# Block sums of a seven-product matmul made by accumulating transfers

## The chip, the cores and the metric

One Trainium2 chip, one of its cores. The metric is the device time of one execution in microseconds, the median over the runs shown. Float32 data; the matmuls are made of three passes over parts of the operands (below).

## The reference

A two-layer decoder trunk on 256 tokens of width 1024. Each layer has a feed-forward block, a mixer (block attention beside a convolution, or a gating unit beside stick-breaking attention) and a second feed-forward block, each between two RMS norms. The change touches the four feed-forward blocks alone, with 2816 hidden columns:

```python
def swiglu(h, w_gate, w_up, w_down):
    return (jax.nn.silu(h @ w_gate) * (h @ w_up)) @ w_down

f = swiglu(rmsnorm(x, g[0]), ffn_w_gate[layer, 0], ffn_w_up[layer, 0], ffn_w_down[layer, 0])
x = x + 0.5 * rmsnorm(f, g[1])
```

## The kernel before

The 256 tokens are two tiles t of 128. The hidden columns are 11 chunks c of 256; a chunk's weights are the gate and the up columns side by side, 1024 rows of 512. `load` brings half a chunk (512 rows) into a buffer `raw` of 128 x 2048 floats, 1 MB, by two transfers from SyncE's queue. There are five raw buffers. `split_raw` makes two units of each: ScalarE copies 1024 columns into `hi` (rounded), VectorE takes the difference into `lo`; there are nine buffers of each. A matmul of the two is three passes on TensorE (hi by hi, hi by lo, lo by hi).

Chunks (2,3), (5,6) and (8,9) of each feed-forward are pairs, 12 in all. For a pair a, b = a + 1 the product is a 2 x 2 block matmul (token tile by row half, row half by chunk) that is made with seven products in place of eight (function `M`, steps i = 0 to 6, one product of 12 matmuls each). The weight blocks are b11, b21 (chunk a, first and second half of the rows) and b12, b22 (chunk b). Four of the seven products take sums of blocks, which VectorE makes in the raw buffers, each 128 x 2048 (lines 358, 359, 374, 382): b12 := b22 - b12, b11 := b12 + b11, then b12 := b22 - b11 and b21 := b21 - b11. The sums of the activations are made once in a feed-forward (`sums`). What the products leave in PSUM is put together by VectorE (u1, u2, c) and goes to `gated`, which applies SiLU on ScalarE and the product on VectorE; then come the transposes (`T`) and the down product (`Dn`, 12 matmuls over a chunk of w_down, whose raw buffer is split in the same way). Tiles X, Y and X2 are PSUM buffers, of which two exist.

A list G of steps is laid out by hand, and `settle` puts T and Dn steps behind the steps that made their chunk. The scheduler of the language sets the order of instructions on each engine from that at build time; each engine runs its own instructions in that order and waits on semaphores. GpSimd issues no transfers: it has the power operation of the norms (line 182), small copies and part of the convolution.

Of the kernel before, what the change touches and what calls it, by code (L numbers as in the profile page):

```python
# [10 lines left out]
F32 = mybir.dt.float32  # L11
# [37 lines left out]
def trunk(ctx, tc, x, norm_g, w_gate, w_up, w_down, ab_in, ab_out, conv_w, conv_b, conv_g, conv_bb,  # L49
# [68 lines left out]
            units += prep(loads, f"gu{l}{j}_{c}_{half}")  # L118
        return [(hi[:, o:o + 512], lo[:, o:o + 512]) for hi, lo in units for o in (0, 512)]

    def load_block(l, j, c, half):

        def loads(raw):
            v = raw.rearrange("p (k g f) -> p k g f", k=4, g=2)
            return [(v[:, :, g, :], w[l, j, half * 512:half * 512 + 512, c * FC:(c + 1) * FC].rearrange("(k p) f -> p k f", p=P))
                    for g, w in ((0, w_gate), (1, w_up))]
        return load(loads, f"b{l}{j}_{c}_{half}")

    def prep_in(w, c, name):
        units = []  # L130
# [119 lines left out]
    def ffn(l, j, pre, tail, hooks=()):  # L250
# [59 lines left out]

        S = {}

        def sums():
            (a11, a12), (a21, a22) = pre[0][3], pre[1][3]
            for n, dst, x, y, op in ((1, a22, a21, a22, ALU.add), (3, a21, a11, a21, ALU.subtract),
                                     (2, a11, a22, a11, ALU.subtract), (4, a12, a12, a11, ALU.subtract)):
                nc.vector.tensor_tensor(dst, x, y, op=op)
                d = sp.tile([P, 8, P], F32R, tag=f"S{n}" if n < 4 else "tg", name=f"S{n}_{l}{j}", bufs=1)  # L320
                split(dst, d[:, 0:4].rearrange("p a b -> p (a b)"), d[:, 4:8].rearrange("p a b -> p (a b)"))
                S[n] = (d[:, 0:4], d[:, 4:8])

# [14 lines left out]
        def M(i, a):  # L338
            b = a + 1
            n = f"{l}{j}_{a}"  # L340
            if i == 0:
                if not S:
                    sums()
                w = W[a] = {}
                w["m"] = sp.tile([P, 2, 512], F32, tag="cacc", name=f"m{n}")
                w["u"] = sp.tile([P, 2, 512], F32, tag="hpad", name=f"u{n}")
                w["b11"] = load_block(l, j, a, 0)
                units = split_raw(w["b11"], f"b11_{n}")
                w["b22"] = load_block(l, j, b, 1)
                w["b12"] = load_block(l, j, b, 0)  # L350
                w["X"] = ps_mm(f"gX{n}")
                product(w["X"], block(0, 0), units, True, False)
                nc.scalar.activation(w["m"][:, 0], w["X"], AF.Copy)
                return
            w = W[a]
            m1, m5, u1, u2 = w["m"][:, 0], w["m"][:, 1], w["u"][:, 0], w["u"][:, 1]
            if i == 1:
                nc.vector.tensor_tensor(w["b12"], w["b22"], w["b12"], op=ALU.subtract)
                nc.vector.tensor_tensor(w["b11"], w["b12"], w["b11"], op=ALU.add)
                units = split_raw(w["b11"], f"t2_{n}")  # L360
                w["b21"] = load_block(l, j, a, 1)
                w["Y"] = ps_mm(f"gY{n}")
                product(w["Y"], S[2], units, True, False)
                nc.vector.tensor_tensor(u1, w["Y"], m1, op=ALU.add)
            elif i == 2:
                units = split_raw(w["b21"], f"b21_{n}")
                product(w["X"], block(0, 1), units, False, True)
                gated(0, a, w["X"])
            elif i == 3:
                units = split_raw(w["b12"], f"t3_{n}")  # L370
                product(w["Y"], S[3], units, False, False)
                nc.vector.tensor_tensor(u2, w["Y"], m1, op=ALU.add)
            elif i == 4:
                nc.vector.tensor_tensor(w["b12"], w["b22"], w["b11"], op=ALU.subtract)  # L374
                units = split_raw(w["b12"], f"t1_{n}")
                w["X2"] = ps_mm(f"gX2{n}")
                product(w["X2"], S[1], units, True, False)
                nc.scalar.activation(m5, w["X2"], AF.Copy)
                nc.vector.tensor_tensor(u2, u2, m5, op=ALU.add)
                gated(1, b, u2)  # L380
            elif i == 5:
                nc.vector.tensor_tensor(w["b21"], w["b21"], w["b11"], op=ALU.subtract)
                units = split_raw(w["b21"], f"t4_{n}")
                product(w["Y"], block(1, 1), units, False, True)
                c = sp.tile([P, 512], F32, tag="va", name=f"c21_{n}", bufs=2)
                nc.vector.tensor_tensor(c, w["Y"], m1, op=ALU.add)
                gated(1, a, c)
            else:
                units = split_raw(w["b22"], f"b22_{n}")
                product(w["X2"], S[4], units, False, True)  # L390
                c = sp.tile([P, 512], F32, tag="va", name=f"c12_{n}", bufs=2)
                nc.vector.tensor_tensor(c, w["X2"], u1, op=ALU.add)
                gated(0, b, c)


        inside = {c for pair in pairs for c in pair}
# [5 lines left out]
            elif (c, c + 1) in pairs:  # L402
                G.extend((M, i, c) for i in range(7))
        G.append((GU, 0, e))
        makes = {2: (0, 0), 4: (1, 1), 5: (1, 0), 6: (0, 1)}
        price = {M: 1.0, GU: 2.0, both: 4.0, T: 0.1, Dn: 1.0}
        total = sum(price[f] for f, _, _ in G if f not in (T, Dn)) + 2
        seq, made, turned_, clock, gone, downs = [], [], [], 0.0, 0.0, 0
# [508 lines left out]
```

## Time and profile before

| | before |
|---|---|
| median of the runs shown | 992.99 us |
| the runs | 993.05, 986.86, 992.99 us |
| profiled execution | 989.26 us, its span 987.3 us |
| TensorE busy | 953.1 us (97%) |
| VectorE busy | 837.7 us (85%) |
| ScalarE busy | 579.4 us (59%) |
| GpSimd busy | 97.7 us (10%) |
| DMA queue of SyncE | 174.50 MB, 53.7% of the 16 engines' span |
| TensorE's granted clock, mean | 0.994 |

PE is TensorE, PEld its weight loads, DVE is VectorE, ACT ScalarE, POOL GpSimd, SP SyncE; a q behind a name is that engine's queue. Times in the trace count from the start of the span. Matmuls overlap in the pipeline, so a matmul's own time is longer than the step from one to the next.

### The profile page before, as it was taken

The page shows a single profiled execution, that of the slowest core. Times are in us where ns is not written, and L with a number is a line of the kernel's source. Part 1 is how long each engine was busy: PE and PEld are TensorE (multiplying, and loading weights), DVE is VectorE, ACT ScalarE, POOL GpSimd, SP SyncE. Part 2 cuts the span into 40 slices and gives each one's busy share as a digit, 9 for nine tenths or more (in the row PEclk, how much of TensorE's full clock was granted, in tenths as well). Part 3 has the DMA queues.
Part 4 walks back from the last instruction along what each step waited for, and adds up shares of the span by engine and source line. Part 5 has one row for each costly group of instructions (what it writes and reads, how often), then busy time and mean ns, then how long its engine had stood idle before and what let it go on. Part 6 is the DMA issues. An engine that isn't in the chain of part 4 may idle for free.

```text
span 987.3 us, 11853 instructions
## 1 busy us (share of the span) xinstructions
PE 953.1 (97%) x4350; PEld 759.0 (77%) x4352; DVE 837.7 (85%) x1022; ACT 579.4 (59%) x845; POOL 97.7 (10%) x104
## 2 busy tenths in 40 slices
PE   7999999999888999999999999999999989999997
PEld 5777888787657688878778887877787778887875
DVE  6999999679887999988789999996757489999883
ACT  7575656563535656656576756575555466656561
POOL 0100000039961000000000000000000010000000
PEclk9999999999989999999999999999999999999999
DMA  9657647456007339383862658385564142838341
GB/s 313 209 184 230 218 167 282 161 177 232 1 18 239 91 107 315 122 262 121 284 213 86 200 183 275 109 311 162 209 220 144 43 127 86 275 120 288 107 168 43
DMA packets 121754, 175.32 MB, mean 178 GB/s; under 512 B 4481, under 2 KB 96321, under 8 KB 121696
## 3 DMA queue, kind: packets, MB, share of 16 engines
q1 hardware_dynamic: 121536, 174.50, 53.7%
q8 instruction: 34, 0.56, 0.2%
q14 instruction: 24, 0.20, 0.1%
q10 hardware_dynamic: 160, 0.07, 0.0%
HBM read 173.50 MB, written 1.05 MB: 177 GB/s over the span
## 4 chain that ended last, share of the span: by engine, by line
PE 84%; DVE 8%; ACT 3%; DMA 2%; issue 2%; POOL 1%; SPq 0%; POOLq 0%; DVEq 0%; ACTq 0%
PE f L145 8%; PE f L146 8%; PE f L147 8%; PE gu L147 6%; PE gu L145 6%; PE gu L146 6%; PE gX L334 4%; PE gX L336 4%; PE gX L335 4%; PE gY L334 3%; PE gY L335 3%; PE gY L336 3%; PE hT L153 2%; PE cd L145 2%; PE cd L146 2%
## 5 line engine op out<-in xcount | busy, mean ns | idle before, releaser
L145 PE MATMUL f<-hi_dn,hs 128*128 128x512 f32 x352 | 139.7, 400 | 0.5 <-ACT hs L157 0.5
L146 PE MATMUL f<-lo_dn,hs 128*128 128x512 f32 x352 | 138.0, 392 | 0.0
L147 PE MATMUL f<-hi_dn,hs 128*128 128x512 f32 x352 | 137.5, 393 | 0.0
L96 ACT ACTIVATE hi_t<-raw_b 128x1024 fp32r<-128x1024 f32 x96 | 98.1, 1053 | 60.2 <-DVE raw_b L374 47.1
L97 DVE TENSOR_TENSOR lo_t<-raw_b,hi_t 128x1024 fp32r<-128x1024 f32 x96 | 114.5, 1220 | 14.5 <-ACT hi_t L96 14.5
L97 DVE TENSOR_TENSOR lo_dn<-raw_dn,hi_dn 128x1024 fp32r<-128x1024 f32 x88 | 105.7, 1219 | 9.0 <-ACT hi_dn L96 8.9
L96 ACT ACTIVATE hi_dn<-raw_dn 128x1024 fp32r<-128x1024 f32 x88 | 91.7, 1055 | 36.4 <-PE gu L147 26.2
L97 DVE TENSOR_TENSOR lo_gu<-raw_gu,hi_gu 128x1024 fp32r<-128x1024 f32 x80 | 96.6, 1218 | 8.3 <-ACT hi_gu L96 8.0
L96 ACT ACTIVATE hi_gu<-raw_gu 128x1024 fp32r<-128x1024 f32 x80 | 83.5, 1055 | 27.9 <-PE m L147 11.7
L97 DVE TENSOR_TENSOR lo_b<-raw_b,hi_b 128x1024 fp32r<-128x1024 f32 x72 | 86.3, 1219 | 2.5 <-ACT hi_b L96 2.3
L96 ACT ACTIVATE hi_b<-raw_b 128x1024 fp32r<-128x1024 f32 x72 | 74.8, 1057 | 21.4 <-PE gu L147 12.9
L145 PEld LDWEIGHTS f<-hi_dn,hs 128*128 128x128 f32 x352 | 65.7, 188 | 17.2 <-ACT hs L157 4.4
L147 PEld LDWEIGHTS f<-hi_dn,hs 128*128 128x128 f32 x352 | 66.1, 188 | 15.3 <-DVE hs L158 1.7
L146 PEld LDWEIGHTS f<-lo_dn,hs 128*128 128x128 f32 x352 | 66.2, 188 | 13.8 <-DVE lo_dn L97 1.0
L157 ACT ACTIVATE hs<-hT 128x256 fp32r<-128x256 f32 x88 | 32.2, 377 | 54.9 <-PE hT L153 54.9
L145 PE MATMUL gu<-hi_gu,xh_l1f 128*128 128x512 f32 x160 | 63.6, 397 | 0.0
L146 PE MATMUL gu<-lo_gu,xh_l1f 128*128 128x512 f32 x160 | 63.4, 396 | 0.0
L147 PE MATMUL gu<-hi_gu,xl_l1f 128*128 128x512 f32 x160 | 62.2, 393 | 0.0
L158 DVE TENSOR_TENSOR hs<-hT,hs 128x256 fp32r<-128x256 f32 x88 | 36.0, 418 | 20.4 <-ACT hs L157 20.0
L282 ACT ACTIVATE sg<-gu 128x256 f32<-128x256 f32 x38 | 14.5, 381 | 42.1 <-PE gu L147 39.3
L334 PE MATMUL gY<-hi_t,S 128*128 128x512 f32 x96 | 38.6, 402 | 0.0
L336 PE MATMUL gY<-hi_t,S 128*128 128x512 f32 x96 | 38.0, 396 | 0.0
(361 smaller groups left out, 2240.7 us busy)
## 6 DMA issues: line engine op xcount, KB each, us to landing
raw_dn<-in_ffn_w_down_dram SPq DMA_DIRECT2D x44, 1024.0 KB, 5.0
raw_b<-in_ffn_w_gate_dram SPq DMA_DIRECT2D x48, 512.0 KB, 4.7
raw_b<-in_ffn_w_up_dram SPq DMA_DIRECT2D x48, 512.0 KB, 6.2
raw_gu<-in_ffn_w_gate_dram SPq DMA_DIRECT2D x38, 512.0 KB, 4.2
raw_gu<-in_ffn_w_up_dram SPq DMA_DIRECT2D x38, 512.0 KB, 5.2
raw_ab<-in_ab_w_in_dram SPq DMA_DIRECT2D x10, 1024.0 KB, 6.9
raw_cd<-in_cd_w_in_dram SPq DMA_DIRECT2D x10, 1024.0 KB, 5.1
raw_abo<-in_ab_w_out_dram SPq DMA_DIRECT2D x4, 1024.0 KB, 5.5
```

The source lines that it names most:

```text
L96: nc.scalar.activation(hi, r, AF.Copy)
L97: nc.vector.tensor_tensor(lo, r, f32v(hi), op=ALU.subtract)
L145: nc.tensor.matmul(ps, xh, wh, start=first, stop=False)
L146: nc.tensor.matmul(ps, xh, wl, start=False, stop=False)
L147: nc.tensor.matmul(ps, xl, wh, start=False, stop=last)
L153: nc.tensor.transpose(ps[:, i * P:(i + 1) * P], src[:, i * P:(i + 1) * P], ident)
L157: nc.scalar.activation(hi, ps, AF.Copy)
L158: nc.vector.tensor_tensor(lo, ps, f32v(hi), op=ALU.subtract)
L282: nc.scalar.activation(sg, ps[:, 0:FC], AF.Silu, scale=1.0 if r is None else r)
L334: nc.tensor.matmul(ps, A[0][:, k, :], wh[:, o], start=first and k == 0, stop=False, **tc_skip)
L335: nc.tensor.matmul(ps, A[0][:, k, :], wl[:, o], start=False, stop=False, **tc_skip)
L336: nc.tensor.matmul(ps, A[1][:, k, :], wh[:, o], start=False, stop=k == 3, **tc_skip)
```

## The change

Of the four sums of blocks of a pair three are made by transfers that add what they bring to what lies in the destination, issued from GpSimd's queue; one stays on VectorE. Blocks and sums have other signs so that all four are additions: t = b12 + b11 (b11 is read from HBM once more), t := t + b22 (VectorE), b22 := b22 + b12 (b12 once more from HBM), b21 := b21 + t (from one raw buffer to another). All four blocks are loaded at the first step, b12 first. The products come in another order: b11, t (b12 + b11), b21, b22, t (with b22), b22 (with b12), b21 (with t). The post-sums and the order in which the outputs are made follow.

```diff
@@ -118,13 +118,21 @@
-    def load_block(l, j, c, half):
+    def block_of(l, j, c, half):
 
         def loads(raw):
             v = raw.rearrange("p (k g f) -> p k g f", k=4, g=2)
             return [(v[:, :, g, :], w[l, j, half * 512:half * 512 + 512, c * FC:(c + 1) * FC].rearrange("(k p) f -> p k f", p=P))
                     for g, w in ((0, w_gate), (1, w_up))]
-        return load(loads, f"b{l}{j}_{c}_{half}")
+        return loads
+
+    def load_block(l, j, c, half):
+        return load(block_of(l, j, c, half), f"b{l}{j}_{c}_{half}")
+
+    def add_block(raw, l, j, c, half):
+
+        for dst, src in block_of(l, j, c, half)(raw):
+            tc.keep_in_program_order(nc.gpsimd.dma_start(dst, src, accum_op=ALU.add))
@@ -310,12 +318,13 @@
-            for n, dst, x, y, op in ((1, a22, a21, a22, ALU.add), (3, a21, a11, a21, ALU.subtract),
-                                     (2, a11, a22, a11, ALU.subtract), (4, a12, a12, a11, ALU.subtract)):
+            for n, dst, x, y, op in ((1, a22, a21, a22, ALU.subtract), (3, a21, a11, a21, ALU.subtract),
+                                     (2, a11, a22, a11, ALU.subtract), (4, a12, a12, a11, ALU.add)):
@@ -338,16 +347,24 @@
+            def made(x, y, op, name):
+                c = sp.tile([P, 512], F32, tag="va", name=f"{name}_{n}", bufs=2)
+                nc.vector.tensor_tensor(c, x, y, op=op)
+                return c
+
             if i == 0:
...
+                w["t"] = load_block(l, j, b, 0)
+                add_block(w["t"], l, j, a, 0)
                 w["b11"] = load_block(l, j, a, 0)
                 units = split_raw(w["b11"], f"b11_{n}")
+                w["b21"] = load_block(l, j, a, 1)
                 w["b22"] = load_block(l, j, b, 1)
-                w["b12"] = load_block(l, j, b, 0)
...
             if i == 1:
-                nc.vector.tensor_tensor(w["b12"], w["b22"], w["b12"], op=ALU.subtract)
-                nc.vector.tensor_tensor(w["b11"], w["b12"], w["b11"], op=ALU.add)
-                units = split_raw(w["b11"], f"t2_{n}")
-                w["b21"] = load_block(l, j, a, 1)
...
+                units = split_raw(w["t"], f"t1_{n}")
+                w["X2"] = ps_mm(f"gX2{n}")
+                product(w["X2"], S[1], units, True, False)
+                nc.scalar.activation(m5, w["X2"], AF.Copy)
...
             elif i == 3:
-                units = split_raw(w["b12"], f"t3_{n}")
+                units = split_raw(w["b22"], f"b22_{n}")
+                nc.vector.tensor_tensor(w["t"], w["t"], w["b22"], op=ALU.add)
+                add_block(w["b22"], l, j, b, 0)
+                tc.keep_in_program_order(nc.gpsimd.dma_start(w["b21"], w["t"], accum_op=ALU.add))
+                product(w["X2"], S[4], units, False, True)
+            elif i == 4:
+                units = split_raw(w["t"], f"t2_{n}")
+                w["Y"] = ps_mm(f"gY{n}")
+                product(w["Y"], S[2], units, True, False)
+                nc.vector.tensor_tensor(u1, w["Y"], m1, op=ALU.add)
+                gated(0, b, made(w["X2"], u1, ALU.subtract, "c12"))
+            elif i == 5:
+                units = split_raw(w["b22"], f"t3_{n}")
                 product(w["Y"], S[3], units, False, False)
                 nc.vector.tensor_tensor(u2, w["Y"], m1, op=ALU.add)
-            elif i == 4:
-                nc.vector.tensor_tensor(w["b12"], w["b22"], w["b11"], op=ALU.subtract)
...
+                nc.vector.tensor_tensor(u2, m5, u2, op=ALU.subtract)
                 gated(1, b, u2)
-            elif i == 5:
-                nc.vector.tensor_tensor(w["b21"], w["b21"], w["b11"], op=ALU.subtract)
+            else:
                 units = split_raw(w["b21"], f"t4_{n}")
                 product(w["Y"], block(1, 1), units, False, True)
...
+                gated(1, a, made(w["Y"], m1, ALU.add, "c21"))
@@ -402,7 +413,7 @@
-        makes = {2: (0, 0), 4: (1, 1), 5: (1, 0), 6: (0, 1)}
+        makes = {2: (0, 0), 4: (0, 1), 5: (1, 1), 6: (1, 0)}
```

## Rows read from the trace of the kernel before

**Rows 1.** The page's busy time, share of the span and instructions of each engine.

```profile
PE 953.1 (97%) x4350; PEld 759.0 (77%) x4352; DVE 837.7 (85%) x1022; ACT 579.4 (59%) x845; POOL 97.7 (10%) x104
```

**Rows 2.** Busy time by stretch: length, engines in order, granted clock, DMA share, GB/s.

```profile
60.00:70.00 10.00, 8.18 (x37) 6.40 (x35) 10.00 (x8) 7.37 (x9) 0.00 (x0) 1.00 0.75 239
...
540.00:550.00 10.00, 10.00 (x45) 8.19 (x44) 9.83 (x10) 6.30 (x7) 0.00 (x0) 1.00 0.01 2
...
590.00:600.00 10.00, 10.00 (x46) 8.18 (x45) 9.50 (x9) 4.87 (x7) 0.00 (x0) 1.00 0.31 100
600.00:610.00 10.00, 10.00 (x47) 7.95 (x46) 9.80 (x12) 7.93 (x10) 0.00 (x0) 1.00 1.04 325
800.00:810.00 10.00, 7.67 (x32) 6.18 (x31) 7.01 (x11) 5.06 (x10) 2.53 (x1) 0.83 0.44 135
```

**Rows 3.** TensorE's waits: waited for, us in total, times, longest.

```profile
PE xT_l1f L153 <- ACT y_l1f L197: 3.3, 3, 2.3
...
PE gY L334 <- ACT hi_t L96: 1.8, 1, 1.8
...
PE gu L145 <- DVE c L392: 0.7, 1, 0.7
```

**Rows 4.** Chain of waits from 55 to 70 us: start, us, what.

```profile
59.55 2.20 DVE raw_b L374
...
62.35 2.21 DVE raw_b L382
```

**Rows 5.** The norms' power operation on GpSimd: ns min/median/max, first and last start.

```profile
L182 POOL TENSOR_TENSOR v_pl1f<-v_pl1f,mhalf x4: 548/548/2529, 501.2 to 801.5; 128x1 f32<-128x1 f32 x4
```

**Rows 6.** Groups by line and shape: count, busy us, mean ns, idle before, releasers.

```profile
L97 DVE TENSOR_TENSOR lo_t<-raw_b,hi_t 128x1024 fp32r<-128x1024 f32 x96 | 114.5, 1220 | 14.5 <-ACT hi_t L96 14.5
...
L96 ACT ACTIVATE hi_t<-raw_b 128x1024 fp32r<-128x1024 f32 x96 | 98.1, 1053 | 60.2 <-DVE raw_b L374 47.1 <-PE f L147 6.1 <-DVE raw_b L359 5.9
...
L97 DVE TENSOR_TENSOR lo_ab<-raw_ab,hi_ab 128x1024 fp32r<-128x1024 f32 x20 | 27.7, 1414 | 2.4 <-ACT hi_ab L96 2.4
L359 DVE TENSOR_TENSOR raw_b<-raw_b,raw_b 128x2048 f32<-128x2048 f32 x12 | 27.5, 2289 | 0.2
```

**Rows 7.** The 1 MB transfers into raw_dn, issue to landing.

```profile
DMA to landing us min/median/max: 4.8/5.0/9.5
```

**Rows 8.** The page's DMA queue of SyncE: packets, MB, share of 16 engines.

```profile
q1 hardware_dynamic: 121536, 174.50, 53.7%
```

**Rows 9.** Timeline of one pair: its first load's issue, its second product's split.

```profile
560.13 0.37 SPq L87 DMA_DIRECT2D raw_b<-in_ffn_w_gate_dram  x1
...
581.80 1.06 ACT L96 ACTIVATE hi_t<-raw_b 128x1024 fp32r<-128x1024 f32 x1
```

**Rows 10.** Timeline of VectorE: fourth splits' ends in four pairs, one last split.

```profile
54.13 2.35 DVE L97 TENSOR_TENSOR lo_t<-raw_b,hi_t 128x1024 fp32r<-128x1024 f32 x2
...
544.77 2.29 DVE L382 TENSOR_TENSOR raw_b<-raw_b,raw_b 128x2048 f32<-128x2048 f32 x1
546.97 1.22 DVE L97 TENSOR_TENSOR lo_t<-raw_b,hi_t 128x1024 fp32r<-128x1024 f32 x1
...
588.87 2.35 DVE L97 TENSOR_TENSOR lo_t<-raw_b,hi_t 128x1024 fp32r<-128x1024 f32 x2
...
609.53 1.22 DVE L97 TENSOR_TENSOR lo_b<-raw_b,hi_b 128x1024 fp32r<-128x1024 f32 x1
...
637.27 2.35 DVE L97 TENSOR_TENSOR lo_t<-raw_b,hi_t 128x1024 fp32r<-128x1024 f32 x2
```

**Rows 11.** Timeline of TensorE: the seventh product's first matmul in these pairs.

```profile
71.13 0.39 PE L334 MATMUL gX<-hi_b,S 128*128 128x512 f32 x1
...
564.09 0.39 PE L334 MATMUL gX<-hi_b,S 128*128 128x512 f32 x1
...
615.19 0.39 PE L334 MATMUL gX<-hi_b,S 128*128 128x512 f32 x1
...
660.88 0.39 PE L334 MATMUL gX<-hi_b,S 128*128 128x512 f32 x1
```

More of the change, by code (lines that the diff above doesn't have):

```diff
@@ L357, in M @@
             if i == 1:
-                nc.vector.tensor_tensor(w["b12"], w["b22"], w["b12"], op=ALU.subtract)
-                nc.vector.tensor_tensor(w["b11"], w["b12"], w["b11"], op=ALU.add)
-                units = split_raw(w["b11"], f"t2_{n}")
-                w["b21"] = load_block(l, j, a, 1)
-                w["Y"] = ps_mm(f"gY{n}")
-                product(w["Y"], S[2], units, True, False)
-                nc.vector.tensor_tensor(u1, w["Y"], m1, op=ALU.add)
+                units = split_raw(w["t"], f"t1_{n}")
+                w["X2"] = ps_mm(f"gX2{n}")
+                product(w["X2"], S[1], units, True, False)
+                nc.scalar.activation(m5, w["X2"], AF.Copy)
             elif i == 2:
@@ L369, in M @@
             elif i == 3:
-                units = split_raw(w["b12"], f"t3_{n}")
+                units = split_raw(w["b22"], f"b22_{n}")
[11 more added lines that the diff above has]
+                units = split_raw(w["b22"], f"t3_{n}")
                 product(w["Y"], S[3], units, False, False)
                 nc.vector.tensor_tensor(u2, w["Y"], m1, op=ALU.add)
-            elif i == 4:
-                nc.vector.tensor_tensor(w["b12"], w["b22"], w["b11"], op=ALU.subtract)
[L375 to L379, printed above, removed]
+                nc.vector.tensor_tensor(u2, m5, u2, op=ALU.subtract)
                 gated(1, b, u2)
-            elif i == 5:
-                nc.vector.tensor_tensor(w["b21"], w["b21"], w["b11"], op=ALU.subtract)
+            else:
                 units = split_raw(w["b21"], f"t4_{n}")
                 product(w["Y"], block(1, 1), units, False, True)
[L385 to L393, printed above, removed]
+                gated(1, a, made(w["Y"], m1, ALU.add, "c21"))
         inside = {c for pair in pairs for c in pair}
```

## The prediction

> **What bounds the kernel now.** I read the page's busy times first: TensorE is busy for 953.1 of 987.3 us, VectorE for 837.7, ScalarE for 579.4, GpSimd for 97.7 [rows 1]. No change to other engines can give back more than TensorE's 34.2 us without work, and much of that lies in the mixers and norms, which the change leaves alone. Next, the busy time by stretch: inside the pairs TensorE is busy for all of 10.00 us while VectorE is busy for 9.5 to 9.83 [rows 2]. So VectorE is nearly full there, but TensorE is full, and TensorE sets the time. Third, who waited for whom: of TensorE's waits only two can go back to what the change removes, 1.8 us behind a split that came late in the very first pair, and 0.7 us behind a post-sum that may have stood behind a block sum on VectorE [rows 3]; I count both as gained. The chain of waits shows the first: two sums of 2.2 us stand one behind the other on VectorE before the split that TensorE waits for [rows 4]; in that stretch TensorE is busy for 8.18 of 10 us [rows 2]. Last the stretch from 800 to 810 us: one GpSimd operation that usually takes 548 ns took 2529 [rows 5], TensorE waited up to 2.3 us for what followed [rows 3], and the granted clock of the stretch is 0.83 [rows 2], so the lower level, 1.2 GHz, held for about 3.4 us and cost 1.7 us more. After the wait of 1.8 us it stayed at 1.00. I take a stall over 2.5 us to cost 1.7 us extra, one under 2 us none.
>
> **What is removed.** Three of four block sums in each of 12 pairs: 36 operations of 2.29 us, 82 us of VectorE [rows 6]; the view has four lines like that one, one for each sum. They stood on VectorE, beside a full TensorE, so nearly all of it is worth nothing; what shows is the 1.8 + 0.7 = 2.5 us of waits. That is the whole gain.
>
> **What is added.** Per pair three accumulates from GpSimd's queue, in five transfers: b11 from HBM onto t (which holds b12), b12 from HBM onto b22, and t from SBUF onto b21, 1 MB each. GpSimd issues no transfer before, so no row prices one. The plain 1 MB transfer lands 4.8 us after issue at the least, 5.0 in the median [rows 7]. The big queue moved 174.50 MB in 53.7% of 987.3 us [rows 8], or 329 GB/s, so 1.05 MB keep the 16 engines busy for 3.2 us and some 1.8 us are latency. An accumulate must also read what it adds to. The lower bound is that this costs nothing; then two accumulates behind each other take 1.8 + 3.2 + 3.2 = 8.2 us. If each byte costs twice, they take 12.8 us on the engines and 1.8 us of latency; three issues at 0.37 us, the price on SP's queue [rows 9], make 1.1, and I round up to 16.0 for the loads beside them. The upper bound is that the three transfers do not overlap and that GpSimd needs 2.5 us for each order, its slowest operation [rows 5]: 3 x (1.8 + 2.5) + 12.8 = 25.7 us. I take 16.0 because reading the destination is real work on the same engines, while nothing shows that the transfers run one by one.
>
> The Trainium skill (Collectives: The Full Stack, The bandwidth ceiling) says that a reducing transfer issues two reads per chunk and so runs at half the rate of a copy, measured there as 1.93; by it the 12.8 us would be 12.4, and no run here shows it yet.
>
> The first accumulate (onto t) has time. A pair's first load is issued at 560.13 and its second product's split begins at 581.80 [rows 9]; t now has that first load, and 21.7 us hold a plain landing of 5 us and an accumulate of 1.8 + 6.4 us, with 8 to spare. I price it at nothing; the first product and the split before it cover it, and if that cover were gone it would cost 8.2 us a pair.
>
> The other two are the ones that count. They can start only when the fourth product's split (of b22) has read b22, and b22 and b21 are due for the sixth and seventh product. So I ask how long the time between is. The end of the fourth split is VectorE's lo operation; the seventh product's first matmul is TensorE's row; a first half of a split takes 1.05 + 1.22 us before it [rows 6]. TensorE's times stay, since it is full.
> - First pair of a feed-forward (three of them alike): the lo ends at 546.97 + 1.22 = 548.2, with a sum of 2.29 ahead of it that is gone, so 545.9 to 546.4 [rows 10]; the seventh product starts at 564.09 [rows 11]. 564.1 - 2.3 - 546.4 = 15.4 us. If the remaining sum (t + b22, 2.29 us) comes behind the split, 13.1. I take the middle, 14.2.
> - The very first pair: 54.13 + 2.35 = 56.5 [rows 10] to 71.13 [rows 11]: 12.3 or 10.1, middle 11.2.
> - Last pairs (four): 637.27 + 2.35 = 639.6 to 660.88 [rows 10, 11]: 19.0 or 16.7, middle 17.8.
> - Middle pairs (four): 588.87 + 2.35 = 591.2 to 615.19: 21.7 or 19.4, middle 20.5.
>
> With 16.0 us the seventh split is late by 1.8 us in three pairs, by 4.8 us in the very first, and in time in eight: 10.2 us. While ScalarE waits for b21, the turned-and-split operations of the down products stand behind it in its queue, so TensorE has nothing to put in the place. Only the 4.8 us stall is over 2.5 and costs 1.7 us of clock. The gain that stays is 0.7 us, for the 1.8 us lies in the pair that is now late. Sum: 10.2 + 1.7 - 0.7 = +11.2 us.
>
> Edits with no price: signs of the post-sums and their order are the same number of VectorE operations of the same shapes; the PSUM buffers X, X2, Y are held as long as before in mirror image. On GpSimd only the next pair's accumulates and the norms' power operations are queued behind an accumulate's wait; the norms come after the last down products, when the pairs are over. VectorE slows beside GpSimd: the same split took 1414 ns in the stretch where GpSimd was busy throughout, and 1220 elsewhere [rows 6]; 16% of VectorE's time in 12 times 16 us is 31 us, hidden in the 82 us freed.
>
> The profiled execution took 989.3 us in all, 2.0 around its span of 987.3; the runs shown are 986.9, 993.0 and 993.1, the median 3.7 above the profiled one. I set the sum on 991, between the two: 991 + 11 = 1002.
>
> **The rivals.**
> - Hidden anyway (not slower). If an accumulate costs little more than a plain transfer (8.2 us) or up to 13 us, every window but the very first pair's holds it, and the kernel gains up to 2.5 us: 988.5. For it: the engines that move data are used at 53.7% [rows 8], at 0.01 to 0.31 where tight and middle windows begin [rows 2]. Against: the destination must be read. It decides below about 14 us.
> - Late in every pair. Midway between 16.0 and 25.7, at 21 us, the lateness is 6.8 in three pairs, 9.8 in the first, 3.2 in four, 0.5 in four: 45; eight stalls over 2.5 us add 13.6 of clock: +58, so 1049. At the upper bound it is 11.5, 14.5, 7.9 and 5.2: 101 and 20 of clock, 1111. For it: 1 KB pieces, and descriptors that GpSimd has to write; against: nothing in the trace shows either as slow.
> - The DMA engines become the bound in bursts. From 590 to 610 us they are busy for 0.31 and 1.04 of the time [rows 2], 13.5 of 20 us; 12.8 more are 6.3 too many. Loads and accumulates then delay each other, and the lead of the last split over its product, 615.2 - (609.5 + 1.2) = 4.4 us [rows 10, 11], covers all but 2. Over eight pairs 16 us, on top of some 10 in the first ones: 1017.
> - GpSimd's norm operations turn slow behind transfers, as the one of 2529 ns [rows 5] did: 2 us and 1.7 of clock at each of four places, 15 us: 1006.
>
> The Trainium skill (DMA: Bandwidth & Descriptors, Issuing engines are not separate DMA queues) says that transfers of all queues run on the same 16 engines and interleave; by that the third rival is a matter of the share left free, which the rows of the stretch give.
>
> **How the numbers follow.** Hidden 0.28; late in the first pairs (the forecast) 0.37; late in every pair 0.17; bursts 0.11; slow norms 0.04; a better order found by chance, over 1% faster, 0.03, since only 2.5 us of waits can go. About 1%, 10 us, is what a measurement here can tell from no change. The forecast's +11 lies at that line; I give 0.20 of its 0.37 to slower. Slower: 0.20 + 0.17 + 0.11 + 0.04 = 0.52; same: 0.28 + 0.17 = 0.45; faster: 0.03. The range runs from 985 (hidden, on a fast run) to 1055 (the nearer half of late in every pair; the farther half, under 0.1, is left out); the forecast alone spans 992 to 1015.
>
> **What would show it.** VectorE's busy time falls by about 82 us to 755, with 12 sums of 2.29 us left. GpSimd's queue shows 60 transfers (five in each of 12 pairs), 38 MB more in all. The waits show ScalarE's hi split standing behind a transfer onto raw_b, and TensorE behind that split, in the four first pairs: then the step on the windows is right. It is wrong if the time from issue to landing of the b22 and b21 accumulates together is under 13 us (hidden) or over 20 (all pairs), if the waits lie at plain loads (bursts), or if t, which I priced at nothing, is the one waited for. A lower granted clock in the middle of a feed-forward would show stalls over 2.5 us.

## The result, and the profile after

The changed kernel takes 1090.95 us (1087.62 to 1098.89) where the one before, beside it, takes 990.88: a ratio of 1.103, 95% interval 1.095 to 1.110. That is 100 us slower, against a forecast of 11 and a range that ended at 1055.

The profiled execution has a span of 1088.4 us against 987.3, 101.1 more. Its page, busy times and queues (as in [rows 1, 8]), and the granted clock (before 0.994):

```profile
PE 981.0 (90%) x4352; PEld 772.1 (71%) x4352; DVE 763.1 (70%) x986; ACT 582.1 (53%) x845; POOL 170.9 (16%) x164
...
q1 hardware_dynamic: 121536, 174.50, 48.0%
q0 software_dynamic: 27072, 37.75, 20.5%
```

```profile
core 0: 1088.4 us, clock 0.965
```

VectorE lost its 36 sums (1022 to 986 operations, 74.6 us of busy time). q0 is GpSimd's new queue. TensorE runs the same matmuls, but its busy time grew from 953.1 [rows 1] to 981.0 us: 27.9 of the 101.1 us are matmuls that run slower, in stretches at the lower clock (13 in the trace against 3 before). Its idle time grew from 34.2 to 107.4 us, by the other 73.2. Nearly all of that is the first three waits below, 72.4 us together; the same three were 0.9 us before. TensorE's and ScalarE's waits after (waited for, us in total, times, longest):

```profile
PE gY L343 <- DVE u L393: 39.0, 12, 9.2
PE f L153 <- ACT hs L165: 17.0, 4, 5.7
PE hT L161 <- DVE h L293: 16.4, 12, 3.6
...
ACT hi_t L96 <- DMA raw_b<-in_ffn_w_up_dram: 59.5, 12, 8.7
ACT hi_dn L96 <- DMA raw_dn<-in_ffn_w_down_dram: 51.5, 8, 8.7
...
ACT hi_t L96 <- DMA raw_b<-raw_b: 29.3, 12, 3.6
```

Below, A is the transfer that makes T1 (b11 onto t), B the one for T3 (b12 onto b22), C the one for T4 (t onto b21). TensorE never waits for T3's or T4's own split here: it waits for hs, h and u, small operations of ScalarE and VectorE. ScalarE waits for B 5 us in each of 12 pairs, for C 2.4, and 51.5 us for down weights, plain loads that wait in line.

A first pair, timeline of all engines (start, length, engine, line, operation; in brackets the idle time before and what ended it):

```profile
391.02 1.30 POOL L135 DMA_DIRECT2D raw_b<-in_ffn_w_gate_dram  x1 [28.92 <-DVE lo_b L97]
...
391.77 1.86 POOL L135 DMA_DIRECT2D raw_b<-in_ffn_w_up_dram  x1
...
392.53 2.01 POOL L387 DMA_DIRECT2D raw_b<-raw_b  x1
...
392.85 0.37 SPq L87 DMA_DIRECT2D raw_gu<-in_ffn_w_gate_dram  x1
...
399.73 0.39 PE L345 MATMUL gX<-hi_b,S 128*128 128x512 f32 x1
403.51 2.00 ACT L96 ACTIVATE hi_t<-raw_b 128x1024 fp32r<-128x1024 f32 x2 [8.66 <-DMA raw_b<-in_ffn_w_up_dram]
...
405.42 0.36 ACT L165 ACTIVATE hs<-hT 128x256 fp32r<-128x256 f32 x1
...
405.83 0.79 PE L153 MATMUL f<-hi_dn,hs 128*128 128x512 f32 x1 [5.71 <-ACT hs L165]
...
408.68 2.00 ACT L96 ACTIVATE hi_t<-raw_b 128x1024 fp32r<-128x1024 f32 x2 [2.90 <-DMA raw_b<-raw_b]
```

T3's split waits for B until 403.51, 12.5 us after its issue. The hs of a down product, whose transposes were done at 397, stands behind it on ScalarE, and TensorE is idle from 400.1 to 405.8. C is there at 408.68, 17.7 us after B's issue. The engines' share in that time (length, engines' busy times, granted clock, DMA share, GB/s):

```profile
389.00:391.00 2.00, 2.00 (x10) 1.65 (x9) 1.67 (x2) 1.93 (x3) 0.00 (x0) 1.00 0.00 0
...
395.00:397.00 2.00, 2.00 (x11) 1.60 (x10) 0.99 (x2) 0.00 (x0) 0.00 (x0) 1.00 1.14 226
...
405.00:407.00 2.00, 1.17 (x2) 0.50 (x2) 2.00 (x3) 0.78 (x2) 0.00 (x0) 0.50 1.02 221
407.00:409.00 2.00, 1.71 (x5) 1.37 (x5) 0.29 (x1) 0.32 (x1) 0.00 (x0) 0.50 0.22 53
```

They are idle before B's issue and for 2 us behind it. From 393 to 407 us they are full, and from 395 on they move 221 to 258 GB/s, where plain loads move 325 at the same share [rows 2, 600 to 610 us]. Then they are nearly idle. B, C and a plain load of 1 MB (raw_gu, 392.85) share them. After the stall the clock is at its lower level, 1.2 GHz.

A middle pair loses its time on VectorE:

```profile
667.35 2.36 DVE L97 TENSOR_TENSOR lo_t<-raw_b,hi_t 128x1024 fp32r<-128x1024 f32 x2 [5.05 <-ACT hi_t L96]
...
672.68 2.36 DVE L97 TENSOR_TENSOR lo_t<-raw_b,hi_t 128x1024 fp32r<-128x1024 f32 x2 [0.38 <-ACT hi_t L96]
...
674.96 0.68 DVE L393 TENSOR_TENSOR u<-gY,m 128x512 f32<-128x512 f32 x1
...
675.70 0.50 PE L343 MATMUL gY<-hi_t,S 128*128 128x512 f32 x1 [3.00 <-DVE u L393]
```

VectorE stands idle for 5.05 us ahead of T3's split, which waits for B, and for 0.38 us ahead of T4's, which waits for C. A split of down weights and T4's then come ahead of u, the sum that must read Y before T3's product may add to it. T3's operand has been ready since 670; TensorE waits 3.0 us for the u behind T4's.

### The profile page after: what moved, and what is told of

The parts are those of the page before. It is cut to its first block, busy times and chain, and to the rows that moved or that the text cites. A ratio compares the mean times of both kernels' runs of the same rounds, so it can differ in the third digit from the quotient of the medians.

```text
span 1088.4 us, 12049 instructions
## 1 busy us (share of the span) xinstructions
PE 981.0 (90%) x4352; PEld 772.1 (71%) x4352; DVE 763.1 (70%) x986; ACT 582.1 (53%) x845; POOL 170.9 (16%) x164
## 3 DMA queue, kind: packets, MB, share of 16 engines
q0 software_dynamic: 27072, 37.75, 20.5%
## 4 chain that ended last, share of the span: by engine, by line
PE 46%; DMA 22%; DVE 19%; ACT 6%; issue 4%; POOL 2%; POOLq 0%; SPq 0%; ACTq 0%; DVEq 0%
DMA raw_b<-raw_b 11%; DMA raw_dn<-in_ffn_w_down_dram 8%; PE gu L154 4%; PE gu L153 4%; PE gu L155 4%; DVE lo_b L97 4%; PE f L155 3%; PE f L153 3%; PE f L154 3%; DMA raw_b<-in_ffn_w_up_dram 3%; DVE lo_t L97 3%; PE gY L343 2%; PE gY L345 2%; DVE lo_dn L97 2%; PE gY L344 2%
## 5 line engine op out<-in xcount | busy, mean ns | idle before, releaser
L153 PE MATMUL f<-hi_dn,hs 128*128 128x512 f32 x352 | 144.7, 415 | 19.7 <-ACT hs L165 17.0
L96 ACT ACTIVATE hi_t<-raw_b 128x1024 fp32r<-128x1024 f32 x96 | 97.7, 1055 | 112.3 <-DMA raw_b<-in_ffn_w_up_dram 59.5
L154 PE MATMUL f<-lo_dn,hs 128*128 128x512 f32 x352 | 143.0, 406 | 0.5 <-DVE lo_dn L97 0.5
L155 PE MATMUL f<-hi_dn,hs 128*128 128x512 f32 x352 | 140.5, 404 | 1.3 <-DVE hs L166 1.3
L96 ACT ACTIVATE hi_dn<-raw_dn 128x1024 fp32r<-128x1024 f32 x88 | 90.1, 1053 | 72.2 <-DMA raw_dn<-in_ffn_w_down_dram 51.5
L97 DVE TENSOR_TENSOR lo_gu<-raw_gu,hi_gu 128x1024 fp32r<-128x1024 f32 x80 | 97.0, 1220 | 34.6 <-ACT hi_gu L96 34.4
L135 POOL DMA_DIRECT2D raw_b<-in_ffn_w_gate_dram x24 | 31.2, 1300 | 510.3 <-DVE lo_b L97 299.7
L153 PEld LDWEIGHTS f<-hi_dn,hs 128*128 128x128 f32 x352 | 69.2, 197 | 37.5 <-ACT hs L165 20.4
L155 PEld LDWEIGHTS f<-hi_dn,hs 128*128 128x128 f32 x352 | 68.8, 195 | 19.0 <-DVE hs L166 4.5
L154 PEld LDWEIGHTS f<-lo_dn,hs 128*128 128x128 f32 x352 | 69.3, 197 | 15.9 <-DVE lo_dn L97 2.3
L343 PE MATMUL gY<-hi_t,S 128*128 128x512 f32 x96 | 42.9, 446 | 39.0 <-DVE u L393 39.0
L343 PEld LDWEIGHTS gY<-hi_t,S 128*128 128x128 f32 x96 | 20.2, 210 | 47.9 <-DVE u L393 34.4
L161 PE MATMUL hT<-cst,h 128*128 128x128 f32 x176 | 36.0, 291 | 17.2 <-DVE h L293 16.4
L165 ACT ACTIVATE hs<-hT 128x256 fp32r<-128x256 f32 x88 | 33.0, 380 | 34.2 <-PE hT L161 33.8
## 6 DMA issues: line engine op xcount, KB each, us to landing
raw_b<-in_ffn_w_up_dram POOLq DMA_DIRECT2D x24, 512.0 KB, 11.4
```

Of the source, the lines that this page charges most:

```text
L96: nc.scalar.activation(hi, r, AF.Copy)
L97: nc.vector.tensor_tensor(lo, r, f32v(hi), op=ALU.subtract)
L135: tc.keep_in_program_order(nc.gpsimd.dma_start(dst, src, accum_op=ALU.add))
L153: nc.tensor.matmul(ps, xh, wh, start=first, stop=False)
L154: nc.tensor.matmul(ps, xh, wl, start=False, stop=False)
L155: nc.tensor.matmul(ps, xl, wh, start=False, stop=last)
```

## The experiments

Each kernel was timed beside the kernel before. "Over before" is (ratio - 1) x 991 us, so that all rows can be compared. "Clock" is the mean granted clock of the profiled execution.

| kernel | A, B, C | us | ratio (95%) | over before | clock |
|---|---|---|---|---|---|
| changed | add, add, add | 1091.0 | 1.103 (1.095 to 1.110) | 102 | 0.965 |
| e1_none | all on VectorE | 996.5 | 1.003 (1.000 to 1.006) | 3 | 0.996 |
| e2_only_A | add, -, - | 1022.6 | 1.029 (1.026 to 1.032) | 29 | 0.983 |
| e3_A_and_B | add, add, - | 1049.0 | 1.056 (1.053 to 1.060) | 56 | 0.978 |
| e4_A_and_C | add, -, add | 1024.8 | 1.032 (1.028 to 1.036) | 32 | 0.989 |
| e5_only_B | -, add, - | 1053.8 | 1.061 (1.056 to 1.066) | 60 | 0.972 |
| e6_only_C | -, -, add | 1021.5 | 1.028 (1.023 to 1.033) | 27 | 0.982 |
| e8_plain_copies | copy, copy, copy | 1008.9 | 1.015 (1.011 to 1.020) | 15 | 0.991 |
| e9_add_A_copy_BC | add, copy, copy | 1022.1 | 1.032 (1.030 to 1.034) | 31 | 0.991 |
| e10_add_B_copy_AC | copy, add, copy | 1048.7 | 1.059 (1.056 to 1.061) | 58 | 0.976 |
| e11_add_C_copy_AB | copy, copy, add | 1033.4 | 1.043 (1.039 to 1.047) | 43 | 0.981 |
| e13_half_adds | half, half, half | 1021.7 | 1.032 (1.029 to 1.035) | 32 | 0.987 |
| e7_splits_in_order | add, add, add | 1103.5 | 1.111 (1.107 to 1.115) | 110 | 0.949 |
| e12_b22_first | add, add, add | 1090.6 | 1.101 (1.099 to 1.103) | 100 | 0.958 |
| e14_downs_later | add, add, add | 1082.8 | 1.094 (1.092 to 1.097) | 93 | 0.962 |
| e16_downs_later_in_order | add, add, add | 1083.7 | 1.092 (1.087 to 1.098) | 91 | 0.959 |
| e17_six_raw | add, add, add | 1082.4 | 1.095 (1.090 to 1.100) | 94 | 0.958 |
| e18_five_raw_eight | add, add, add | 1093.7 | 1.106 (1.103 to 1.109) | 105 | 0.962 |

**Transfers back to VectorE, in the new order of products (e1 to e6).** e1 makes these three edits; e2 to e6 make those of the transfers that they leave out:

```diff
-                add_block(w["t"], l, j, a, 0)
...
+                nc.vector.tensor_tensor(w["t"], w["t"], w["b11"], op=ALU.add)
                 units = split_raw(w["t"], f"t1_{n}")
...
-                add_block(w["b22"], l, j, b, 0)
-                tc.keep_in_program_order(nc.gpsimd.dma_start(w["b21"], w["t"], accum_op=ALU.add))
...
-                units = split_raw(w["b22"], f"t3_{n}")
+                nc.vector.tensor_tensor(w["b11"], w["t"], w["b11"], op=ALU.subtract)
+                units = split_raw(w["b11"], f"t3_{n}")
...
+                nc.vector.tensor_tensor(w["b21"], w["b21"], w["t"], op=ALU.add)
                 units = split_raw(w["b21"], f"t4_{n}")
```

> The changed kernel's order of products, its signs and its early loads, with all sums made by VectorE again: b12 += b11 for T1, += b22 for T2, b11 := T2 - b11 for T3, b21 += T2 for T4; no transfer comes from GpSimd's queue. If the transfers' lateness is the whole loss (theory 'late transfers'): 985 to 998 us, VectorE's busy time back at about 838 us. If the new order of the products loses time by itself, three Y products in a row with a sum of VectorE between each two of them (theory 'order'): 1005 us or more, with the wait of the Y product's matmul for u still among TensorE's waits at over 20 us. If it is that four blocks of a pair are loaded at its first product, so that the down weights come late (theory 'buffers'): 1005 to 1030 us with waits for the down weights and none for u.

> As e1_none, but T1 is made by the accumulating transfer (b11 from HBM onto b12); T2, T3 and T4 are sums of VectorE. By the prediction T1's transfer costs nothing: within 4 us of e1_none, VectorE's busy time 27 us less (12 sums of 2.28 us). If the doubled bytes delay the other loads of the pair, or the accumulate lands after ScalarE comes to the split of T1: 10 to 30 us above e1_none, with T1's split waiting for GpSimd's queue.

> T1 and T3 by accumulating transfers, T4 a sum of VectorE. Theory 'late transfers', lateness counted from the place that T3's split has in ScalarE's order: B lands about 12 us after its issue in the four first pairs and holds up a split of hs, 5.7 us each, and pushes two spells of clock: 20 to 45 us above e2_only_A, and the wait of Y's matmul for u falls from 39 us to under 10, since T4's split waits for no transfer. If C, not B, is what is felt: within 8 us of e2_only_A.

> T1 and T4 by accumulating transfers, T3 a sum of VectorE (T2 - b11). C starts without B ahead of it and has about 8 us of bytes instead of 16 with B, so it lands some 9 us after its issue. Theory 'late transfers': if C's lateness behind B is what VectorE waits for, it is mostly gone: 0 to 15 us above e2_only_A. If a transfer from SBUF to SBUF is slow by itself, or VectorE comes to T4's lo split well before: 30 to 60 us above e2_only_A with the wait for u still at 20 us or more.

> T3 alone by accumulating transfer (b12 from HBM onto b22), T1, T2 and T4 sums of VectorE. Theory 'burst': T1's transfer costs 26 us because its doubled bytes fall on the stretch in which the pair's four blocks and the down weights are loaded; B is issued after that stretch, so it costs less: 1000 to 1010 us, all of it the four holds of hs at 5.5 to 6 us in the first pairs. Theory 'additive', each transfer from HBM costs its 26 us wherever it stands: 1018 to 1028 us.

> T4 alone by accumulating transfer (T2 onto b21, SBUF to SBUF), all other sums by VectorE. It cost 2 us with T1's transfer there. Theory 'latency only': C alone lands some 8 us after its issue, ahead of T4's split: 994 to 1002 us, no wait for u above 10 us. If a transfer between SBUF and SBUF costs by itself: over 1005 us.

e1 costs 3 us: signs, order of products and early loads are next to free, and the theories "order" and "buffers" fall as causes by themselves. VectorE is busy for 837.5 us again. Its wait for u:

```profile
PE gY L343 <- DVE u L391: 6.1, 4, 1.8
```

Any one transfer loses 24 us or more over e1: A 26, C 24, B 57. B alone was expected at 1000 to 1028 us and took 1053.8; C alone at 994 to 1002 or over 1005, and took 1021.5. e3's time was as expected, but its wait for u, expected under 10 us, was 24.3 with no late C in it. The prices do not add up: A costs 26 us alone, 5 with C there (e4 against e6), and takes 4 off with B there (e3 against e5). When a sum moves, the instructions behind it move too (between the traces of e1 and e5, 99 of TensorE's 4352 matmuls stand in another place), so these six can't be summed. The next four can.

**The same order, adds turned into copies (e8 to e11).** On every engine these kernels have the changed kernel's instructions in the same order; where a transfer only copies, its sum is left out. e8 (e9 to e11 turn back one transfer each into an add):

```diff
-            tc.keep_in_program_order(nc.gpsimd.dma_start(dst, src, accum_op=ALU.add))
+            tc.keep_in_program_order(nc.gpsimd.dma_start(dst, src))
...
-                tc.keep_in_program_order(nc.gpsimd.dma_start(w["b21"], w["t"], accum_op=ALU.add))
+                tc.keep_in_program_order(nc.gpsimd.dma_start(w["b21"], w["t"]))
```

> The three transfers stay in place, in GpSimd's queue and with the same waits, but copy without adding, so T1, T3 and T4 are b11, b12 and T2: that part of the result is left out. Theory 'twice the wire': the queue's share of the engines halves (20.5% to about 10%), B lands some 8 us after its issue instead of 12: 1015 to 1050 us. Theory 'issue and waits', the cost is GpSimd's 1.3 to 2.0 us for each issue, the latency and the order, not the bytes: 1070 to 1095 us.

> The changed kernel's instructions in the same order on every engine; T1's transfer adds, T3's and T4's only copy, so that part of the result is left out. With all three copying it was 1008.9 us, with all three adding 1091.0: 82 us are to be shared out. By the prediction T1's doubled bytes cost nothing: 1007 to 1013 us. By the single undoings (26 us for T1's transfer alone, with the down weights' split waiting 57.7 us): 1025 to 1037 us, and ScalarE's wait for the down weights back at about 50 us from 19.

> Same order on every engine; only T3's transfer adds, T1's and T4's copy. ScalarE's wait for B was 59.5 us with adding and 28.8 with copying. Theory 'B's own lateness': TensorE's wait for hs at the down products comes back (17 us in four first pairs) with its clock: 1030 to 1050 us. Theory 'only the sum of B and C is felt': the split of T4 is what holds the path, and B adds its 3 us per pair to C's landing: 1040 to 1055 us with the wait for u at over 25 us.

> Same order on every engine; only T4's transfer adds, T1's and T3's copy. C's bytes then follow B's half as long and land about 12 us after B's issue, some 2 us later than with all copies and 3 to 5 us sooner than with all adding. T4's split comes 2 us later: if u stands behind it, 2 to 3 us a pair in 12 pairs, 1020 to 1040 us, with the wait for u at 15 to 30 us. If T4's split has 4 us of slack there: 1008 to 1015 us.

Copies cost 15 us over before, adds 102: 87 us are the adding. e8 took 1008.9 us, below both its expectations (1015 to 1050, and 1070 to 1095) and nearer the one on bytes. Turned on one by one, A costs 31 - 15 = 16, B 43, C 28, together 87. By the intervals of the table each price is known to some 5 or 6 us and the whole to 8 or 9; within that the three simply add. (A by itself, expected at 1007 to 1013 us or at 1025 to 1037, took 1022.1.) e8's queue, waits, GpSimd's issues (busy us, mean ns), then the issue of the same line in the changed kernel:

```profile
q0 software_dynamic: 8640, 37.75, 11.3%
```

```profile
PE gY L343 <- DVE u L393: 11.5, 8, 3.3
...
ACT hi_t L96 <- DMA raw_b<-in_ffn_w_up_dram: 28.8, 12, 3.7
...
ACT hi_dn L96 <- DMA raw_dn<-in_ffn_w_down_dram: 19.0, 6, 4.2
```

```profile
L135 POOL DMA_DIRECT2D raw_b<-in_ffn_w_up_dram x24 | 18.0, 750 | 5.6 <-DMA raw_b<-in_ffn_w_up_dram 4.4 <-issue 1.3
```

```profile
L135 POOL DMA_DIRECT2D raw_b<-in_ffn_w_up_dram x24 | 39.7, 1655 | 0.7 <-issue 0.7
```

Copies move 37.75 MB in 11.3% of 1009.4 us, 331 GB/s; adds take 20.5% of 1088.4, 169 GB/s: 1.96 times as long. What each transfer does, from the waits of e9 (A adds), e10 (B adds) and e11 (C adds):

```profile
PE hT L161 <- DVE h L293: 10.4, 12, 2.3
...
ACT hi_dn L96 <- DMA raw_dn<-in_ffn_w_down_dram: 49.9, 9, 8.2
```

```profile
PE gY L343 <- DVE u L393: 27.2, 12, 7.7
PE f L153 <- ACT hs L165: 16.8, 4, 5.7
...
ACT hi_t L96 <- DMA raw_b<-in_ffn_w_up_dram: 62.1, 12, 8.6
```

```profile
PE gY L343 <- DVE u L393: 27.5, 10, 6.4
...
ACT hi_t L96 <- DMA raw_b<-raw_b: 28.6, 10, 5.1
```

A does not delay its own sum but the down weights behind it: 49.9 us of ScalarE's waits against 19.0. On TensorE it shows as the wait for h, 10.4 us against 4.0 in e8. B is what hs waits for: 16.8 us in e10, 0.9 in e8. B and C each bring the wait for u. How A does it, in two windows and one row of the timeline of e9:

```profile
943.00:945.00 2.00, 2.00 (x10) 1.65 (x10) 0.66 (x1) 1.06 (x1) 0.00 (x0) 1.00 1.16 239
945.00:947.00 2.00, 2.00 (x11) 1.65 (x10) 0.57 (x1) 0.00 (x0) 0.00 (x0) 1.00 1.11 385
```

```profile
951.13 2.01 ACT L96 ACTIVATE hi_dn<-raw_dn 128x1024 fp32r<-128x1024 f32 x2 [6.82 <-DMA raw_dn<-in_ffn_w_down_dram]
```

At 943 to 945 us the engines are full and move 239 GB/s, with adds among the loads; from 945 on, as the last of A ends (it lands at 947.4), 385. The down weights, in line there, are split at 951.13.

**As many bytes as the copies, but added (e13).**

```diff
-            tc.keep_in_program_order(nc.gpsimd.dma_start(dst, src, accum_op=ALU.add))
+            tc.keep_in_program_order(nc.gpsimd.dma_start(dst[:, 1:3], src[:, 1:3], accum_op=ALU.add))
...
-                tc.keep_in_program_order(nc.gpsimd.dma_start(w["b21"], w["t"], accum_op=ALU.add))
+                tc.keep_in_program_order(nc.gpsimd.dma_start(w["b21"][:, 512:1536], w["t"][:, 512:1536], accum_op=ALU.add))
```

> The changed kernel with as many transfers, each adding, but each over half of its block only (two of the four row groups of the weight blocks, half of T2's columns), so the engines carry as many bytes for them as in the kernel in which all three copy; the sums are left out for the other half. Theory 'bytes': the time is that of the copies, 1003 to 1016 us. Theory 'the add itself', a transfer that adds has a delay of its own whatever its size: 1040 us or more, T3's and T4's splits some 12 and 17 us after B's issue in the first pairs as with whole adds.

```profile
q0 software_dynamic: 14784, 18.88, 11.4%
```

The order of the instructions is the changed kernel's but for a few. The queue takes the copies' share, 11.4%, and the kernel is 32 us over before: 70 of the 87 us go with the bytes on the engines. It came between its two expectations, at 1021.7 us: 17 us over the copies stay, with GpSimd's records of issuing half an add at 1211 to 1912 ns in the mean against 547 to 761 for a whole copy, and 14784 packets against 8640. Which of these the 17 us are isn't settled.

**Where the lateness is felt (e7, e12, e14, e16).** e7 ties the splits of T3 and T4 to their place in the program:

```diff
-                units = split_raw(w["b22"], f"t3_{n}")
+                units = split_raw(w["b22"], f"t3_{n}", tc.keep_in_program_order)
...
-                units = split_raw(w["b21"], f"t4_{n}")
+                units = split_raw(w["b21"], f"t4_{n}", tc.keep_in_program_order)
```

e12 exchanges the third and fourth products of a pair, and their loads, which was to issue B a product earlier. e14 lets the planner put no down product directly behind the second to fourth:

```diff
-            if (f, t, c) not in ((GU, 0, e), (GU, 0, 0)) and (first or (f, t, c) != (GU, 0, 1)):
+            if (f, t, c) not in ((GU, 0, e), (GU, 0, 0)) and not (f is M and t in (1, 2, 3)) and (first or (f, t, c) != (GU, 0, 1)):
```

e16 is e7 and e14 together.

> The changed kernel with all three transfers; only the splits of T3 and T4 are tied to their place in the program, behind what stands before them on ScalarE and VectorE, so that u and hs no longer stand behind a split that waits for a transfer. Theory 'what stands behind the wait': TensorE's wait for u (39 us) and for hs at the down products (17 us) fall to under 15 us together, and with them most of the spells of half clock: 1035 to 1060 us; what is left is T1's 26 us and the down weights. Theory 'the products themselves wait for the transfers': the waits only move to T3's and T4's own products, 1075 to 1100 us.

> All three transfers add, and the result is whole; the products of b21 and b22 change places (and their loads), so that B is issued one product earlier, 5 us and a down product's time where one stands between; C is issued about where it was. Theory 'window': T3's wait for B (59.5 us) goes and C's bytes no longer stand behind B's, so that C lands 8 to 9 us after its issue: 1035 to 1060 us, what is left being T1's transfer and the down weights. Theory 'the engines are full anyway': B's bytes now fall on the loads of the pair and of the down weights: 1075 us or more.

> All three transfers add, the result is whole; the planner puts no down product behind the second, third and fourth products of a pair, so these come between T2's and T3's products and T3's product has one more down product (2.6 us of TensorE) behind B's issue in 11 of the 12 pairs. A product or a down product is 12 matmuls of 0.213 us, 2.6 us; the 5 us named for b22's earlier product were twice that. Theory 'window': each pair gets up to 2.6 us back, and the clock with it: 1045 to 1068 us. Theory 'what stands ahead in ScalarE's and VectorE's order': the splits still hold hs and u, as their place among these engines' instructions is not moved: 1080 us or more.

> The two edits e7_splits_in_order and e14_downs_later together: down products stand between T2's and T3's products, and the splits of T3 and T4 stay behind the hs, u and sg that precede them in the program. Theory 'both conditions': lateness is felt where a waiting split stands ahead of other work, and where it does not, where TensorE's work runs out; with work there and the splits in place, T3's product waits for next to nothing and the hs wait (39 us in e14) goes to under 15 us: 1040 to 1066 us. Theory 'the transfers' bytes set the pace whatever the order': 1075 us or more, the waits only named otherwise.

TensorE's waits in e7; in e12; in e14, with its timeline of a first pair; in e16, with one of ScalarE's:

```profile
PE hT L161 <- DVE h L293: 34.2, 13, 5.1
PE gY L344 <- DVE lo_t L97: 11.6, 16, 0.8
PE gY L343 <- ACT hi_t L96: 11.3, 8, 1.4
```

```profile
PE gY L343 <- DVE h L293: 55.9, 12, 4.9
```

```profile
PE f L153 <- ACT hs L165: 39.1, 13, 5.1
```

```profile
397.10 2.01 ACT L96 ACTIVATE hi_t<-raw_b 128x1024 fp32r<-128x1024 f32 x2 [4.74 <-DMA raw_b<-in_ffn_w_up_dram]
...
403.22 1.06 ACT L96 ACTIVATE hi_t<-raw_b 128x1024 fp32r<-128x1024 f32 x1 [2.21 <-DMA raw_b<-raw_b]
...
404.18 0.36 ACT L165 ACTIVATE hs<-hT 128x256 fp32r<-128x256 f32 x1
...
404.60 0.79 PE L153 MATMUL f<-hi_dn,hs 128*128 128x512 f32 x1 [4.18 <-ACT hs L165]
```

```profile
PE f L153 <- ACT hs L165: 24.8, 24, 3.4
PE hT L161 <- DVE h L293: 19.4, 15, 2.6
...
ACT hi_t L96 <- DMA raw_b<-in_ffn_w_up_dram: 55.2, 12, 5.6
```

None gave back over 11 us, and the intervals of e14 and e16 still meet the changed kernel's; in all four the wait for u is at most 1.3 us. e7 is no faster: with the splits late in the order, ScalarE waits for neither B nor C any longer, but T3's and T4's products wait for their own splits (22.9 us), and the transposes for h (34.2 us). At 1103.5 us it is just over both expectations.

Neither e12 nor e14 made the window longer, the time from B's issue to T3's product. In the traces 794 matmuls stand between the two in the changed kernel, over all twelve pairs and without the small transposes; in e12 there are 792, in e14 784. e12 (whose expectation took a product of under 3 us for 5) besides gives Y the PSUM buffer of X, which h now frees just ahead of it: 55.9 us of waiting that the exchange itself brought. In e14 T2's product moved ahead of a down product, and that is all: T3's product waits neither for its split nor for u, but hs now stands behind T4's split, which waits for C (403.22 to 404.18). So the loss moved from u to hs, and a longer window is untested.

e16 was to take both away, and did not: ScalarE still waits for B in all twelve pairs, 55.2 us, with hs behind it. Its 1083.7 us lie on the side of "the bytes set the pace whatever the order", but it doesn't show that, since its order still has the waiting split ahead of other work. What these runs show is that a waiting split holds whatever stands behind it.

**Raw buffers (e17, e18).** One raw buffer more for one split buffer less, against that split buffer less alone:

```diff
-NW = 9
-NRAW = 5
+NW = 8
+NRAW = 6
```

> The changed kernel with six raw buffers in place of five; the room comes from one less buffer for splits (eight of each, hi and lo). Its partner with five raw and eight split buffers, e18_five_raw_eight, has the same instructions in the same order on TensorE, VectorE, ScalarE and GpSimd. Theory 'buffers couple the transfers to the pace': T3's and T4's raw buffers stay occupied until the slow adds have landed and are split, SyncE waits 103 us for T4's, the engines' load stands idle ahead of the adds (share 0.00 from 389 to 393 us) and is full behind them; a sixth buffer lets the next loads go ahead: 25 us or more below the partner. Theory 'only the adds' own lateness': the next loads are not what is late, and earlier ones share the engines with the adds: within 8 us of the partner.

> The partner: the changed kernel with five raw buffers and eight split buffers of each kind. If the ninth split buffer does nothing: 1085 to 1100 us; if a split waits for a buffer: 1100 us or more.

e18 is where it was expected if the ninth split buffer does nothing. Against it the sixth raw buffer is worth 11 us, between the two expectations. ScalarE's wait for the down weights and TensorE's for h, in e18:

```profile
ACT hi_dn L96 <- DMA raw_dn<-in_ffn_w_down_dram: 30.6, 6, 7.7
...
PE hT L161 <- DVE h L293: 11.6, 8, 3.1
```

In e17 they are 16.1 and 1.1 us. TensorE's wait for u stays (39.8 and 43.7 us). So the buffers carry a tenth of the loss, that of the down weights, and not the sums' lateness.

## Why the prediction was wrong, step by step

**The price of two adds was right.** T = 16.0 us stood for B and C; from B's issue to T4's split it was 17.2 to 17.7 in the four first pairs and 13.8 to 15.0 in the other eight. The part on the engines, 12.8 us, is 12.4 by q0's 169 GB/s; the issues lie 0.75 us apart, not 0.37. In the first pair shown a plain load follows B's issue after 1.8 us, in the middle one after 5.4; that this makes the first pairs longer is likely, not shown. The Trainium skill (Collectives: The Full Stack, The bandwidth ceiling) has a reducing transfer between cores at half the rate of a copy, measured as 1.93; q0's rows agree for adds on one core, at 1.96. The upper bound, transfers one by one, did not hold: B, C and a plain load ran together. With these measured times in the prediction's windows the lateness would be 16 us in place of 10.2, so T is not what failed.

**"I price it at nothing" failed, for A: 16 us (e9).** I asked whether A lands before its own sum is split; it does, 6 to 9 us before. I did not ask what stands behind it on the engines, and that is the down weights. The rival on bursts had this mechanism, but for B and C; that its 1017 us is near the 1022 of A alone is luck.

**The windows failed, and they were the core of the sum.** Three things were wrong in one step. I judged only the seventh product, by C, and never asked when B is there for the sixth; ScalarE waits twice as long for B (59.5 us) as for C (29.3), and B costs 43 us. I counted to the time at which TensorE needs the operand, although the change leaves the split where it stood, ahead of that need on engines that run in order: what is late is what stands behind it. I had that thought for the down products only ("stand behind it in its queue") and used it as a reason why TensorE has nothing else to do, not as the point from which lateness counts. And I took eight pairs to be in time; u is waited for in all twelve.

**"Edits with no price"** was right by itself (e1: 3 us) and wrong in company: the new order puts u between T2's and T3's products, and u is what a late split on VectorE holds. 39.0 us, and 6.1 where no transfer is late.

**The clock was mis-sized.** One stall at 1.7 us was in the sum; TensorE's busy time grew by 27.9 us, since there were many stalls and the lower level lasted longer behind them: 6.8 us behind the stall of 5.7.

**Right were** the gain (next to nothing: VectorE's 74.6 us free no one), the 60 transfers and 38 MB, and the first pairs as the worst: TensorE's long stalls behind hs lie in three of them, 5.4 to 5.7 us each where 1.8 were forecast, and the very first loses 9.2 us behind u where 4.8 were. Together they are 26 us and their clock, of 101. Of the rivals, "late in every pair" had the place, all 12 pairs, and its 1049 to 1111 us hold the 1091; that is luck too, for it needs a T of 21 to 25.7, and T was never over 17.7. VectorE's slowing beside GpSimd, 31 us said to be hidden, did not show: the split that took 1220 ns [rows 6] took 1221.

**What stays open.** The runs show that 87 of the 102 us are the adding, 70 of them by e13 with its bytes, and the trace shows the waits at which the changed kernel loses them. Four other orders lost about as much at other waits; but none of them made the window longer, and e7, which took the waits for B and C off ScalarE, put the splits too late for their own products. Whether some order hides the adds is open. The 12 us between e8's copies and e1, and the 17 us of e13, are not taken apart.

## What to carry to other kernels

Work that leaves a nearly full engine is worth nothing while another engine is the bound; what replaces it is not free merely because its own result is early enough. Ask of each new transfer two things: which loads stand behind its bytes on the engines, and where its reader stands in an in-order engine's program. And to price parts of a change, turn them off without moving anything else: copies in place of adds gave three prices that sum to the whole within their error, undoing the parts gave prices that do not. And before a run is read as a test of an order, count in its trace whether the order is what it was meant to be.

## What the runs showed of the hardware

- By the time that their packets took on the 16 engines, accumulating transfers moved 169 GB/s (changed kernel) and the same transfers, copying, 331 (e8), all three together.
- GpSimd's record of issuing an accumulate lasted 1.3 to 2.0 us in the mean against 0.55 to 0.76 for a copy, and half the bytes hardly shortened it (1.2 to 1.9). The issues of B and C nevertheless began some 0.75 us apart, adding (391.02, 391.77, 392.53) as copying. SyncE's record for a load of 0.5 MB lasted 0.37 us [rows 9].
- Adds from HBM were cut finer: A or B each bring 9216 more packets than as copies (17856 against 8640), C none (8640), and yet C's time on the engines grows too (q0 13.6% of 1032.0 us, against 11.3% of 1009.4).
